# Order of the small matmuls in the head-group stage, and the queue that fetches its modulation weights

## The chip, the cores and the metric

The kernel runs on one core of a Trainium2 chip. The metric is device time in microseconds (us) of one execution. The engines are TensorE (PE, whose weight loads are listed as PEld), VectorE (DVE), ScalarE (ACT), GpSimd (POOL) and SyncE (SP, which here only issues DMAs; its issuing is listed as SPq). TensorE works on the data at the clock that the profile lists as granted, as a share of full speed.

## The reference

One layer of a decoder with a prompt of 512 tokens and eight single-token samples, width 2048, 32 heads of 64. Sixteen heads are dilated sliding-window softmax attention, sixteen are RWKV-7 heads. For the prompt an RWKV head runs this recurrence over all 512 tokens:

```
def step(S, inp):
    r_t, w_t, k_t, v_t, a_t, b_t = inp
    sa = jnp.einsum('bhij,bhj->bhi', S, a_t)
    S = S * w_t[:, :, None, :] + sa[..., None] * b_t[:, :, None, :] + v_t[..., None] * k_t[:, :, None, :]
    return S, jnp.einsum('bhij,bhj->bhi', S, r_t)
...
mix = jnp.concatenate([att, rw], axis=-1) @ P['w_out'][l]
x = x + gt1[:, None, :] * mix
h2 = modulate(rmsnorm(x, P['norm2_g'][l]), sh2, sc2)
```

Ahead of it stand a modulated norm and one input projection, behind it the output projection and a SwiGLU network. The factors `gt1`, `sh2`, `sc2` (and the rest of the modulation) are a projection of the condition `c` by `ada_w`, 2048 x 12288.

## The kernel before

The input projection, the output projection and the feed-forward network run as stages of their own. Between the first two lies the **head-group stage**, about 900 to 1527 us into the profiled execution. The change lies in it alone.

The stage treats heads in pairs, two heads on the two halves of 64 partitions: eight RWKV pairs and eight attention pairs. An RWKV pair (`rwkv_pair`) is cut into 8 chunks of 64 tokens. Its steps follow each other:

- `pg`: 16 matmuls of 64 rows give the products of every chunk's tokens (two banks of 512 columns for each head). VectorE masks each bank into `GM`.
- SyncE writes parts of `GM` to DRAM (`nd`) and reads them back in another layout (`i`). VectorE inverts all 16x16 diagonal blocks at once (`itmp`, `xi`, 19 instructions or so, each needing the last). SyncE writes the result to DRAM (`xd`) and reads it back as `XX`.
- GpSimd masks `E` out of `GM`. Then come short matmuls that double the block size of the inverse twice: `pq`, `px`, `pxt` (64x64, eight for each half) and `pq`, `px` with 32x32 blocks (in the program `pq2`, `px2`), with copies on ScalarE and sums on VectorE between them.
- `pat`, `pgv`, `pu`, `pxa` apply the inverse to the values and make the matrices `Mt` that carry the state from chunk to chunk.

The pair's `chain` then walks over the chunks (`pch`), and makes the outputs (`zy`, `z2`). An attention pair (`attn_pair`) computes scores `pz`, their transposes `pzt` and the values `po` of the prompt, and the samples' attention from the cache (`K` multiplied on GpSimd, `pov` on TensorE).

Beside this the stage makes the 16 blocks 8 to 23 of the modulation (`ada_steps`): each takes four transfers of 1 MiB of `ada_w` into one of two buffers `raw_ada`, 16 matmuls against `c_st`, and a sum. The call of `AQ.dma_start` at L236 issues the transfers; `AQ` is SyncE's queue.

A scheduler sets the order of each engine's instructions, from the order of calls (a string of steps such as `f2 r0 r1 c0 a0 f3 r2 c1`, where r is an RWKV pair, c its chain, a an attention pair and f some modulation blocks), and from when buffers come free; chains have a priority. The eight PSUM banks of the stage are divided up as: `pa` one bank (all `pg`), `psa` two (`pq` to `pxa`, used in turn), `pst` two (attention), one each for chains, samples and modulation. A matmul with 64 rows or 64 columns uses one half of the array. In the code a loop over `c` or `h` runs over the halves.

Of the kernel before, what the change touches and what calls it, by code (L numbers as in the profile page):

```python
# [12 lines left out]
ALU = mybir.AluOpType  # L13
# [65 lines left out]
def hymba_step(tc, a):  # L79
# [97 lines left out]
    with ExitStack() as top:  # L177
# [627 lines left out]
        with ExitStack() as wk_stack:  # L805
# [58 lines left out]
            copies = lambda name: wk.tile([P, 512], F32, tag="adac", name=name, bufs=1)  # L864
            todo += [ada_steps(b, raws, psd_, copies, SPL, PER) for b in range(ADA, ADB)]
# [13 lines left out]
            def rwkv_pair(pr):  # L879
# [88 lines left out]
                for c in range(2):  # L968
                    top_, bot = slice(c * 64, c * 64 + 32), slice(c * 64 + 32, c * 64 + 64)
                    for i in range(8):  # L970
                        mm(pq2[bot, i, :32], gm(i // 2, c, i % 2, top_, slice(c * 64 + 32, c * 64 + 64)), X2T[top_, i, :32])
                Q2 = tq2(f"Q2{pr}", 256).rearrange("p (i t) -> p i t", i=8)
                px2 = psa(f"px2{pr}").rearrange("p (i t) -> p i t", i=8)
                for c in range(2):
                    top_, bot = slice(c * 64, c * 64 + 32), slice(c * 64 + 32, c * 64 + 64)
                    ac.copy(Q2[bot], pq2[bot, :, :32])
                    for i in range(8):
                        mm(px2[top_, i, :32], Q2[bot, i, :], X2[bot, i, 32:])
                    ve.tensor_copy(X2[top_, :, 32:], px2[top_, :, :32])
# [11 lines left out]
                for c in range(2):  # L991
                    for b in range(4):
# [16 lines left out]
                Mt = wl.tile([P, 4, 2, E], F32, tag="mt", name=f"Mt{pr}", bufs=NMT)  # L1009
                for c in range(2):  # L1010
                    pxa = psa(f"pxa{pr}{c}")
                    for i in range(8):
                        o_ = i // 2 * 64
                        mm(pxa[hb[i % 2], o_ : o_ + 64], AG[hb[c], i, 1, :], X2[hb[c], i, :])
                    for i in range(8):
                        b, h = i // 2, i % 2
                        o_ = 256 + b * 64
# [448 lines left out]
```

## Time and profile before

| | us |
|---|---|
| median of three runs | 3356.26 |
| lowest and highest | 3343.64, 3372.01 |
| the profiled execution, its own time | 3378.55 |
| its span | 3376.8 |
| head-group stage in it | about 900 to 1527 |
| granted TensorE clock of the profiled execution, mean | 0.918 |

The profiled execution lies 22 us above the median of the runs, and its span lacks 1.8 us of its own time. TensorE is busy for 88% of the span, VectorE for 73%, ScalarE for 38%, GpSimd for 6%. A matmul is recorded as two or more passes, so a row's number of matmuls is twice that of the program's or more.

### The profile page before, as it was taken

What the parts mean: (1) busy time and instruction counts of PE and PEld (TensorE: products, weight loads), DVE (VectorE), ACT (ScalarE), POOL (GpSimd) and SP (SyncE); (2) the same over time, 40 slices, a digit from 0 to 9 for tenths busy, and PEclk for the clock granted to TensorE, in tenths of its full rate; (3) what the DMA queues carried; (4) which work ended last, traced back from release to release, by engine and by line L of the source; (5) the groups of instructions that cost most, each with busy time, mean ns of one, the idle gap of its engine ahead of it and who ended that gap; (6) DMA issues with size and microseconds to landing.
All of it is one profiled execution on the core that took longest, in us unless ns stands there. A gap on an engine that the chain in (4) does not pass through costs nothing.

```text
span 3376.8 us, 59004 instructions
## 1 busy us (share of the span) xinstructions
PE 2981.6 (88%) x23282; PEld 2629.4 (78%) x23282; DVE 2480.9 (73%) x4846; ACT 1278.0 (38%) x2041; POOL 212.9 (6%) x216
## 2 busy tenths in 40 slices
PE   6987888999889999977977999999999987888988
PEld 2477787889746666656967999999999987787878
DVE  5666788777557455656878787778777788889786
ACT  3353343334223343444434333333333343334333
POOL 0100122110012111101000000000000000000000
PEclk8978999999858798887988999999999998999999
DMA  7744444444579798933322333333333332323223
GB/s 255 232 139 154 147 159 157 133 146 140 175 223 282 201 239 232 249 103 117 109 78 69 113 104 104 108 112 107 113 101 113 109 125 96 99 94 119 85 94 104
DMA packets 449194, 476.17 MB, mean 141 GB/s; under 512 B 84110, under 2 KB 360547, under 8 KB 448916
## 3 DMA queue, kind: packets, MB, share of 16 engines
q1 hardware_dynamic: 438736, 452.16, 43.4%
q10 hardware_dynamic: 7428, 11.65, 1.0%
q0 software_dynamic: 2752, 8.60, 0.8%
q8 instruction: 182, 2.98, 0.4%
q14 instruction: 96, 0.79, 0.1%
HBM read 409.10 MB, written 68.17 MB: 141 GB/s over the span
## 4 chain that ended last, share of the span: by engine, by line
PE 35%; DVE 28%; DMA 23%; issue 5%; ACT 5%; SPq 1%; POOL 1%; ACTq 0%; DVEq 0%; POOLq 0%
PE ada L90 4%; DMA raw_ada<-in_ada_w 2%; SPq L130 1%; PE po L90 1%; DVE x_a L125 1%; PE lx L90 1%; PE pg L90 1%; PE pz L90 1%; PE px L90 1%; DMA K<-in_cache_k 1%; PE pch L90 1%; PE pq L90 1%; DMA xb<-in_ada_w 1%; PE q22M L90 1%; PE q31M L90 1%
## 5 line engine op out<-in xcount | busy, mean ns | idle before, releaser
L90 PE MATMUL ada<-raw_ada,c_st 128*32 128x512 f32 x584 | 123.7, 763 | 17.5 <-DMA raw_ada<-in_ada_w 16.8
L90 PE MATMUL ada<-xb,c_st 128*32 128x512 f32 x184 | 69.9, 673 | 15.9 <-DMA xb<-in_ada_w 13.8
L1037 ACT ACTIVATE Sall<-pch,ppl 64x64 f32<-64x64 f32 x128 | 39.5, 309 | 75.5 <-PE pch L90 57.7
L1238 POOL TENSOR_TENSOR K<-K,qb 128x1024 f32<-128x1024 f32 (+2 forms) x24 | 58.2, 2440 | 147.5 <-DMA K<-in_cache_k 91.6
L1188 ACT ACTIVATE z<-z,mx 128x128 f32<-128x128 f32 (+3 forms) x64 | 35.8, 560 | 78.2 <-DVE mx L1187 37.9
L90 PEld LDWEIGHTS pg<-AR,BK 64*128 64x128 f32 x256 | 41.0, 237 | 22.7 <-issue 11.9
L90 PE MATMUL pz<-ak,aq 64*128 64x256 f32 (+3 forms) x128 | 55.3, 581 | 0.7 <-DMA ak<-pqd 0.7
L90 PE MATMUL pg<-AR,BK 64*128 64x128 f32 x256 | 49.1, 342 | 6.1 <-DMA AR<-abd 2.7
L90 PE MATMUL g0M<-x_g,g0hl 128*128 128x260 f32 x168 | 31.3, 348 | 21.7 <-ACT x_g L124 7.4
L90 PE MATMUL po<-zt,av 128*64 128x128 f32 x320 | 49.1, 310 | 0.4 <-ACT zt L1200 0.4
L90 PE MATMUL o0M<-x_m,o0hl 128*128 128x260 f32 x168 | 33.5, 366 | 17.6 <-ACT x_m L124 14.2
L901 DVE TENSOR_TENSOR GM<-pg,cst 128x512 f32<-128x512 f32 x32 | 22.0, 688 | 36.5 <-PE pg L90 36.3
L198 PEld LDWEIGHTS pzt<-ident,z 128*128 128x128 f32 x160 | 19.0, 155 | 37.5 <-ACT z L1190 13.0
L1184 DVE SCALAR_TENSOR_TENSOR z<-pz,rnq,T 128x128 f32<-128x128 f32 (+3 forms) x64 | 34.4, 546 | 18.3 <-PE pz L90 16.2
L90 PEld LDWEIGHTS g0M<-x_g,g0hl 128*128 128x128 f32 x168 | 27.5, 241 | 25.4 <-ACT x_g L124 8.7
L90 PEld LDWEIGHTS o0M<-x_m,o0hl 128*128 128x128 f32 x168 | 29.7, 259 | 21.6 <-ACT x_m L124 17.5
L1412 DVE SCALAR_TENSOR_TENSOR y<-c_d,modT,y 128x512 f32<-128x512 f32 x64 | 45.9, 751 | 0.0
L90 PEld LDWEIGHTS ada<-raw_ada,c_st 128*32 128x32 f32 x584 | 16.4, 119 | 37.4 <-DMA raw_ada<-in_ada_w 22.7
L1200 ACT COPY zt<-pzt 128x128 f32<-128x128 f32 (+3 forms) x64 | 26.5, 426 | 49.5 <-PE pzt L198 41.1
L90 PEld LDWEIGHTS po<-zt,av 128*64 128x64 f32 x320 | 34.2, 151 | 13.3 <-issue 6.8
L198 PE MATMUL pzt<-ident,z 128*128 128x128 f32 x160 | 33.8, 321 | 11.8 <-ACT z L1190 10.0
L1190 ACT ACTIVATE z<-z,mx 128x128 f32<-128x128 f32 (+3 forms) x64 | 35.5, 559 | 16.8 <-DVE mx L1189 11.6
(2104 smaller groups left out, 9215.3 us busy)
## 6 DMA issues: line engine op xcount, KB each, us to landing
raw_ada<-in_ada_w SPq DMA_DIRECT2D x64, 1024.0 KB
xb<-in_ada_w SPq DMA_DIRECT2D x92, 256.0 KB
actd<-c_u SPq DMA_DIRECT2D x22, 520.0 KB
a<-actd SPq DMA_DIRECT2D x22, 520.0 KB
raw_ada<-in_ada_w SPq DMA_DIRECT2D x36, 256.0 KB
lsd<-lx SPq DMA_DIRECT2D x12, 520.0 KB
prd<-rkv SPq DMA_DIRECT2D x24, 256.0 KB
K<-in_cache_k SPq DMA_DIRECT2D x16, 384.0 KB
```

What stands on the lines that cost most here:

```text
L90: pe.matmul(out, lhsT=lhsT, rhs=rhs, start=start, stop=stop)
L125: ve.tensor_sub(x[:, 1, o:e], src, x[:, 0, o:e].bitcast(F32))
L130: sp.dma_start(raw.rearrange("p (k m) c -> p k (m c)", k=2), src[k * P : (k + 2) * P, :].rearrange("(k p) m -> p k m", p=P))
L198: pe.transpose(out, in_=in_, identity=ident[:n, 0:n])
L901: ve.tensor_tensor(GM[i][:, :, :, h], pg, gmask.unsqueeze(2).to_broadcast([P, 2, 2, P]), op=ALU.mult)
L1037: ac.activation(S[hb[h], ch + 1, hb[h]], pc_[hb[h], ch, :], AF.Copy, scale=ppl[hb[h], pr, ch : ch + 1])
L1184: ve.scalar_tensor_tensor(z, in0=pz[:, :nk], scalar=rn[:, qi, h : h + 1], in1=Ts[h][:, 384 - 128 * qi :], op0=ALU.mult, op1=ALU.add)
L1188: ac.activation(z, z, AF.Exp, bias=mx[:, 0:1], accum_out=mx[:, 1:2])
L1190: ac.activation(z, z, AF.Copy, scale=mx[:, 2:3])
L1200: ac.copy(zt, pzt[:, :nk])
L1238: OK.tensor_mul(K[:n], K[:n], qb[:n])
L1412: ve.scalar_tensor_tensor(y[:, f, :SEQ], in0=c[:, j, :SEQ], scalar=modT[:, 48 + f, 0:1], in1=y[:, f, :SEQ], op0=ALU.mult, op1=ALU.add)
```

## The change

Three things are different, all in the head-group stage.

1. The loops of most small matmuls are turned inside out, so that matmuls for the two halves follow each other in turn (`pg`, `pq`, `px`, `pxt`, `pq2`, `px2`, `pat`, `pgv`, `pu`, `pxa`, `z2`, `pz`, `po`). The number and sizes of matmuls stay as they are.
2. For that, two banks are needed at once where one was: `pg` of the second head comes from `psa` (`pa` still serves the first), both `pxa` banks are taken before the first `pxa` matmul, both `pz` before the first score.
3. `AQ` is GpSimd's queue from this stage on.

```
+            AQ = gp
             todo += [ada_steps(b, raws, psd_, copies, SPL, PER) for b in range(ADA, ADB)]
...
                 for i in range(2):
+                    pg = [f(f"pg{pr}{i}{h}").rearrange("p (b c t) -> p c b t", b=2, c=2) for h, f in enumerate((pa, psa))]
+                    for b in range(2):
+                        for c in range(2):
+                            cc = slice((4 * i + 2 * b + c) * 128, (4 * i + 2 * b + c + 1) * 128)
+                            for h in range(2):
+                                mm(pg[h][:, c, b, :], BK[hb[h], cc], AR[hb[h], cc])
                     for h in range(2):
-                        rows = slice(h * 64, h * 64 + 64)
-                        pg = pa(f"pg{pr}{i}{h}").rearrange("p (b c t) -> p c b t", b=2, c=2)
-                        for b in range(2):
-                            for c in range(2):
-                                cc = slice((4 * i + 2 * b + c) * 128, (4 * i + 2 * b + c + 1) * 128)
-                                mm(pg[:, c, b, :], BK[rows, cc], AR[rows, cc])
-                        ve.tensor_tensor(GM[i][:, :, :, h], pg, gmask.unsqueeze(2).to_broadcast([P, 2, 2, P]), op=ALU.mult)
+                        ve.tensor_tensor(GM[i][:, :, :, h], pg[h], gmask.unsqueeze(2).to_broadcast([P, 2, 2, P]), op=ALU.mult)
...
-                for c in range(2):
-                    for i in range(8):
+                for i in range(8):
+                    for c in range(2):
                         mm(pq[hb[c], i, :], E1f[hb[c], i, :], XX[1][hb[c], i, :])
...
+                pxa = [psa(f"pxa{pr}{c}") for c in range(2)]
+                for i in range(8):
+                    o_ = i // 2 * 64
+                    for c in range(2):
+                        mm(pxa[c][hb[i % 2], o_ : o_ + 64], AG[hb[c], i, 1, :], X2[hb[c], i, :])
...
                 def scores(qi):
                     nk = 128 * (qi + 1)
+                    pzs = [pst(f"pz{pr}{h}{qi}") for h in range(2)]
                     for h in range(2):
-                        hr = slice(h * 64, h * 64 + 64)
-                        pz = pst(f"pz{pr}{h}{qi}")
-                        mm(pz[:, :nk], q[hr, qi * 128 : (qi + 1) * 128], kn[hr, :nk])
+                        mm(pzs[h][:, :nk], q[hb[h], qi * 128 : (qi + 1) * 128], kn[hb[h], :nk])
+                    for h in range(2):
                         z = tz(f"z{pr}{h}{qi}", nk)
...
                     po = pst(f"po{pr}{qi}")
-                    for h in range(2):
-                        hr = slice(h * 64, h * 64 + 64)
-                        for j in range(qi + 1):
-                            mm(po[hr, :128], vt_[:, j, hr], zts[qi, h][:, j * 128 : (j + 1) * 128], start=(j == 0), stop=(j == qi))
+                    for j in range(qi + 1):
+                        for h in range(2):
+                            mm(po[hb[h], :128], vt_[:, j, hb[h]], zts[qi, h][:, j * 128 : (j + 1) * 128], start=(j == 0), stop=(j == qi))
```

The scheduler makes a new order for every engine out of this. The stage has 2,778 matmul instructions in both programs. Those whose predecessor uses a part of the array that they don't touch, before and after: `pq` (64x64) 11 and 120 of 128, `px` 12 and 124, `pxt` 3 and 126, `pgv` 16 and 123, `pu` 25 and 122, `pat` 10 and 56 of 64, `po` 24 and 119 of 160, `z2` 56 and 115 of 128. For `pg` it is 8 and 9 of 128 and for `pz` 21 and 20 of 64, so that these two stay as they were. The last of the 64 modulation transfers is used by the stage's 2,535th matmul before and by its 1,645th after.

On TensorE, where pair 0 ends and pair 1 is in its inversion, before (digits behind a name are the pair, then the bank and the head or half: `pg210` is pair 2, bank 1, head 0):

```order
L90 MATMUL pxa01_9440<-X20_9310,AG0_9366 64x64 x8
L90 MATMUL pxa01_9440<-BKt0_9353,XA0_9395 64x64 x8
L90 MATMUL ada10_10064<-sel4_67,adac10_10089 128x9 x4
L90 MATMUL pg210_10164<-AR2_10141,BK2_10142 128x128 x4
L90 MATMUL pz113_10747<-ak1_10646,aq1_10645 128x512
L198 MATMUL pzt102_10756<-ident_63,z102_10706 128x128 x3
L90 MATMUL pq1_9535<-XX11_9523,E11_9530 64x64 x8
L90 MATMUL pch0_9737<-Sall0_9132,Mt0_9420 64x64 x2
L90 MATMUL pq1_9535<-XX11_9523,E11_9530 64x64 x8
L90 MATMUL ada11_10096<-raw_ada11_0_10097,c_st_82 32x512 x4
L90 MATMUL ada11_10096<-raw_ada11_4_10103,c_st_82 32x512 x4
L90 MATMUL pg211_10170<-AR2_10141,BK2_10142 128x128 x4
```

The `pg` of pair 2 are done between the `pq` of pair 1. The same stretch of pair 2 after, at the end of pair 1:

```order
L90 MATMUL pxa11_9700<-BKt1_9631,XA1_9673 64x64
L198 MATMUL pzts1_10830<-ident_63,zs1_10825 97x16
L90 MATMUL ada14_10918<-raw_ada14_12_10937,c_st_82 32x512 x4
L90 MATMUL po20_11419<-zt210_11417,av2_11366 64x128
L90 MATMUL pz202_11423<-ak2_11365,aq2_11364 128x384
L90 MATMUL pov1_10839<-V10_10840,pts_10831 32x256 x4
L90 MATMUL pov1_10839<-V11_10846,pts_10831 32x256 x4
L90 MATMUL pov1_10839<-V12_10852,pts_10831 32x256 x4
L90 MATMUL pg201_10153<-AR2_10141,BK2_10142 128x128
L90 MATMUL pch1_10419<-Sall1_9133,Mt1_9698 64x64 x2
L90 MATMUL pg201_10153<-AR2_10141,BK2_10142 128x128 x3
L90 MATMUL pg211_10165<-AR2_10141,BK2_10142 128x128 x4
```

The second head's `pg` of pair 2 (`pg201`, `pg211`) now stand behind the last `pxa` of pair 1, since their bank is one of the two that pair 1 uses in turn up to `pxa`. In every later pair it is so too.

On VectorE, around the start of the 16x16 inversion of pair 4, before:

```order
L1062 TENSOR_TENSOR Y2_11325<-Y2_11325,z220_11335 128x256
L979 COPY X23_11092<-px23_11114 32x8x32
L926 TENSOR_TENSOR itmp4_11725<-i164_11721,xi4_11723 64x2
L928 TENSOR_REDUCE xi4_11723<-itmp4_11725 64x2
L926 TENSOR_TENSOR itmp4_11725<-i164_11721,xi4_11723 64x2x4
L928 TENSOR_REDUCE xi4_11723<-itmp4_11725 64x2x2
L926 TENSOR_TENSOR itmp4_11725<-i164_11721,xi4_11723 64x2x9
L1050 TENSOR_TENSOR UV2_10146<-UV2_10146,zy21_11345 64x2x128 x2
L928 TENSOR_REDUCE xi4_11723<-itmp4_11725 64x2x3
L979 COPY X23_11092<-px23_11114 32x8x32
L1270 COPY mixs_78<-pov2_11558 64x4 x4
L926 TENSOR_TENSOR itmp4_11725<-i164_11721,xi4_11723 64x2x16
```

Instructions of pair 2's chain, pair 3's inversion and the samples stand between those of the inversion. After:

```order
L902 TENSOR_TENSOR GM41_11692<-pg411_11706,cst_9118 128x4x128
L248 TENSOR_TENSOR modT_69<-ada21_12389,adab_72 128x36
L250 TENSOR_SCALAR modT_69<-modT_69 128x36
L1212 COPY at4_12809<-po43_12948 128x128
L927 TENSOR_TENSOR itmp4_11725<-i164_11721,xi4_11723 64x2
L929 TENSOR_REDUCE xi4_11723<-itmp4_11725 64x2
L927 TENSOR_TENSOR itmp4_11725<-i164_11721,xi4_11723 64x2x4
L929 TENSOR_REDUCE xi4_11723<-itmp4_11725 64x2x2
L927 TENSOR_TENSOR itmp4_11725<-i164_11721,xi4_11723 64x2x9
L929 TENSOR_REDUCE xi4_11723<-itmp4_11725 64x2x3
L927 TENSOR_TENSOR itmp4_11725<-i164_11721,xi4_11723 64x2x16
L929 TENSOR_REDUCE xi4_11723<-itmp4_11725 64x2x4
```

The inversion's instructions follow each other with nothing between.

On GpSimd, around the masking of `E` for pair 2 (`E12` in the rows), before:

```order
L1136 TENSOR_TENSOR tm3_10607<-T5_10542,dv_10550 128x1024
L1238 TENSOR_TENSOR K10_10805<-K10_10805,qb1_10801 128x1024
L1238 TENSOR_TENSOR K11_10811<-K11_10811,qb1_10801 96x1024
L1053 MEMSET Y1_10503 64x128
L948 TENSOR_TENSOR E12_10212<-GM20_10150,cst_9118 64x256
L948 TENSOR_TENSOR E12_10212<-GM21_10151,cst_9118 64x256
L948 TENSOR_TENSOR E12_10212<-GM20_10150,cst_9118 64x256
L948 TENSOR_TENSOR E12_10212<-GM21_10151,cst_9118 64x256
L1238 TENSOR_TENSOR K12_10817<-K12_10817,qb1_10801 97x1024
L1053 MEMSET Y2_11325 64x128
```

It stands among other multiplies and clears, and after it stands between DMA issues of `raw_ada`, each of which needs one of the two buffers to come free:

```order
L236 DMA raw_ada16_4_11612<-in_ada_w 128x4x512
L1243 TENSOR_TENSOR K22_11536<-K22_11536,qb2_11520 97x1024
L236 DMA raw_ada16_8_11618<-in_ada_w 128x4x512
L1059 MEMSET Y2_11325 64x128
L236 DMA raw_ada16_12_11624<-in_ada_w 128x4x512
L949 TENSOR_TENSOR E12_10212<-GM20_10150,cst_9118 64x256
L949 TENSOR_TENSOR E12_10212<-GM21_10151,cst_9118 64x256
L949 TENSOR_TENSOR E12_10212<-GM20_10150,cst_9118 64x256
L949 TENSOR_TENSOR E12_10212<-GM21_10151,cst_9118 64x256
L236 DMA raw_ada17_0_11638<-in_ada_w 128x4x512
```

The masks of `E` and the samples' multiplies `K` are now queued behind those issues.

## Rows read from the trace of the kernel before

**Rows 1.** The page's head: span of the profiled execution.

```profile
span 3376.8 us, 59004 instructions
```

**Rows 2.** Windows: stretch, length, busy PE, PEld, DVE, ACT, POOL, PEclk, DMA share, GB/s.

```profile
900.00:1520.00 620.00, 555.56 (x5251) 376.36 (x5251) 349.95 (x851) 230.43 (x615) 95.77 (x76) 0.79 0.79 222
915.00:1300.00 385.00, 348.80 (x3211) 232.17 (x3211) 223.90 (x538) 136.51 (x365) 66.27 (x51) 0.77 0.87 241
1200.00:1250.00 50.00, 45.75 (x473) 32.30 (x474) 27.77 (x70) 22.08 (x62) 10.47 (x8) 0.97 1.00 259
1373.00:1422.00 49.00, 44.58 (x517) 30.80 (x516) 31.77 (x77) 19.93 (x59) 10.86 (x9) 0.87 0.90 248
```

**Rows 3.** Timeline: last `Mt` of pairs 0 and 7.

```profile
1030.83 0.42 DVE L1020 TENSOR_TENSOR Mt<-pxa,eye 128x256 f32<-128x256 f32 x1
...
1481.74 0.42 DVE L1020 TENSOR_TENSOR Mt<-pxa,eye 128x256 f32<-128x256 f32 x1
```

**Rows 4.** Timeline of RWKV pair 6, from its last `pg` to its `Mt`.

```profile
1320.75 0.42 PE L90 MATMUL pg<-AR,BK 64*128 64x128 f32 x1
...
1325.47 0.60 SPq L915 DMA_DIRECT2D i<-nd  x1
...
1330.08 0.15 DVE L926 TENSOR_TENSOR itmp<-i,xi 64x2 f32<-64x2 f32 x1
...
1347.93 0.36 DVE L938 COPY xi<-xi 64x256 f32<-64x256 f32 x1
...
1349.29 0.84 SPq L941 DMA_DIRECT2D xd<-xi  x1
...
1361.81 4.60 SPq L944 DMA_DIRECT2D XX<-xd  x2
...
1421.95 0.42 DVE L1020 TENSOR_TENSOR Mt<-pxa,eye 128x256 f32<-128x256 f32 x1
```

**Rows 5.** Timeline, TensorE: start, length, engine, line, matmul, form, number of records.

```profile
1202.92 1.31 PE L90 MATMUL pu<-AG,X 64*64 64x128 f32 x14
...
1208.85 0.68 PE L90 MATMUL pxa<-X,AG 64*64 64x64 f32 x16
...
1209.37 0.46 PE L90 MATMUL pxa<-BKt,XA 64*64 64x64 f32 x10
...
1237.74 1.09 PE L90 MATMUL po<-zt,av 128*64 128x128 f32 x8
...
1248.01 0.70 PE L90 MATMUL pz<-ak,aq 64*128 64x256 f32 x2
...
1372.76 1.85 PE L90 MATMUL pq<-XX,E 64*64 64x64 f32 x32
...
1383.95 0.70 PE L90 MATMUL pz<-ak,aq 64*128 64x256 f32 x4
```

**Rows 6.** Groups of matmuls by form, 900 to 1520: busy, mean ns, idle before.

```profile
L90 PE MATMUL pg<-AR,BK 64*128 64x128 f32 x256 | 49.1, 342 | 6.1 <-DMA AR<-abd 2.7 <-DVE GM L901 2.1 <-DVE rb L857 0.8
L90 PE MATMUL po<-zt,av 128*64 128x128 f32 x320 | 49.1, 310 | 0.4 <-ACT zt L1200 0.4
L90 PE MATMUL px<-XX,Q 64*64 64x64 f32 x256 | 40.5, 267 | 0.1
L90 PE MATMUL pu<-AG,X 64*64 64x128 f32 x256 | 20.5, 275 | 0.0
```

**Rows 7.** Windows, VectorE's instructions on tile `xi` alone: busy, PEclk, DMA share, GB/s.

```profile
1330.00:1348.30 18.30, 8.11 (x19) 1.00 0.93 279
```

**Rows 8.** Waits of SyncE's queue, 900 to 1520: total, times, longest.

```profile
SPq L236 <- PE ada L90: 87.2, 28, 10.3
```

**Rows 9.** GpSimd's DMA issues of the next stage: duration ns min/median/max.

```profile
L1321 POOL DMA_DIRECT2D mix<-mixd x8: 722/722/790, 1529.1 to 1560.3; - x8
```

More of the change, by code (lines that the diff above doesn't have):

```diff
@@ L958, in rwkv_pair @@
                 pxt = psa(f"pxt{pr}").rearrange("p (i t) -> p i t", t=E)
-                for c in range(2):
-                    for i in range(8):
+                for i in range(8):
+                    for c in range(2):
                         mm(px[hb[c], i, :], Q[hb[c], i, :], XX[0][hb[c], i, :])
+                for i in range(8):
+                    for c in range(2):
                         mm(pxt[hb[c], i, :], XX[0][hb[c], i, :], Q[hb[c], i, :])
@@ L990, in rwkv_pair @@
                 pat = psa(f"pat{pr}")
-                for c in range(2):
-                    for b in range(4):
+                for b in range(4):
+                    for c in range(2):
                         mm(pat[hb[c], b * 128 : (b + 1) * 128], ARv[:, b, 3 * c, :], ident)
@@ L995, in rwkv_pair @@
                 pgv = psa(f"pgv{pr}")
-                for c in range(2):
-                    for i in range(8):
+                for i in range(8):
+                    for c in range(2):
                         mm(pgv[hb[c], i * 64 : i * 64 + 64], gm(i // 2, c, i % 2, hb[1 - c], hb[c]), UV[hb[1 - c], i // 2 * 2 + c, i % 2, :])
@@ L1002, in rwkv_pair @@
                     pu = psa(f"pu{pr}{q}").rearrange("p (b h x e) -> p b h x e", b=2, h=2, x=2)
-                    for c in range(2):
-                        for i in range(4):
+                    for i in range(4):
+                        for c in range(2):
                             mm(pu[hb[c], i // 2, i % 2], X2[hb[c], 4 * q + i, :], AG[hb[c], 4 * q + i])
@@ L1009, in rwkv_pair @@
                 Mt = wl.tile([P, 4, 2, E], F32, tag="mt", name=f"Mt{pr}", bufs=NMT)
-                for c in range(2):
[L1011 to L1017, printed above, removed]
-                        mm(pxa[hb[h], o_ : o_ + 64], XA[hb[c], b, h, :], BKt[hb[c], 2 * b + c, h * 64 : h * 64 + 64])
-                    ac.copy(ARv[:, :, 3 * c, :], pxa[:, :256].rearrange("p (b t) -> p b t", b=4))
-                    ve.tensor_tensor(Mt[:, :, c, :], pxa[:, 256:].rearrange("p (b t) -> p b t", b=4),
+                pxa = [psa(f"pxa{pr}{c}") for c in range(2)]
+                for i in range(8):
+                    o_ = i // 2 * 64
+                    for c in range(2):
+                        mm(pxa[c][hb[i % 2], o_ : o_ + 64], AG[hb[c], i, 1, :], X2[hb[c], i, :])
+                for i in range(8):
+                    b, h = i // 2, i % 2
+                    o_ = 256 + b * 64
+                    for c in range(2):
+                        mm(pxa[c][hb[h], o_ : o_ + 64], XA[hb[c], b, h, :], BKt[hb[c], 2 * b + c, h * 64 : h * 64 + 64])
+                for c in range(2):
+                    ac.copy(ARv[:, :, 3 * c, :], pxa[c][:, :256].rearrange("p (b t) -> p b t", b=4))
+                    ve.tensor_tensor(Mt[:, :, c, :], pxa[c][:, 256:].rearrange("p (b t) -> p b t", b=4),
                                      eye2.unsqueeze(1).to_broadcast([P, 4, E]), op=ALU.add)
@@ L1057, in chain @@
                     z2 = psz(f"z2{pr}{q}").rearrange("p (b e) -> p b e", b=4)
-                    for c in range(4):
+                    for n in range(8):
+                        c, h = n // 4 * 2 + n % 2, n // 2 % 2
                         b, R_ = 2 * q + c // 2, hb[1 - c % 2]
-                        for h in range(2):
-                            mm(z2[R_, c // 2, h * 64 : h * 64 + 64], gm(b, c % 2, h, slice(0, 128), R_), UV[:, 4 * q + c, h, :])
+                        mm(z2[R_, c // 2, h * 64 : h * 64 + 64], gm(b, c % 2, h, slice(0, 128), R_), UV[:, 4 * q + c, h, :])
                     ve.tensor_add(Y[:, q2], Y[:, q2], z2[:, :2])
@@ L1202, in values @@
                     po = pst(f"po{pr}{qi}")
-                    for h in range(2):
-                        hr = slice(h * 64, h * 64 + 64)
-                        for j in range(qi + 1):
-                            mm(po[hr, :128], vt_[:, j, hr], zts[qi, h][:, j * 128 : (j + 1) * 128], start=(j == 0), stop=(j == qi))
+                    for j in range(qi + 1):
+                        for h in range(2):
+                            mm(po[hb[h], :128], vt_[:, j, hb[h]], zts[qi, h][:, j * 128 : (j + 1) * 128], start=(j == 0), stop=(j == qi))
                     ve.tensor_copy(at[:, qi * 128 : (qi + 1) * 128], po[:, :128])
```

17 lines of the change are left out of this document (9 added, 8 removed).

## The prediction

> **What bounds the kernel now.** I read the page's head first [rows 1], then the windows of the head-group stage [rows 2], since the change lies there alone. From 900 to 1520 us TensorE is busy for 555.6 of 620 us at a mean granted clock of 0.79; VectorE is busy for 350, ScalarE for 230, GpSimd for 96, and the DMA engines for a share of 0.79. So TensorE is nearly full, and it is the first candidate. But it is nearly full with three kinds of work (RWKV pairs, attention, modulation) that cover each other's waits, and the stage also has a cadence: the last `Mt` of pair 0 is made at 1030.83 and that of pair 7 at 1481.74 [rows 3], which is 450.9 / 7 = 64.4 us for a pair. The third view is one pair's own path [rows 4]. In pair 6 the last `pg` ends at 1321.2, the first `pq` starts at 1372.8, and `Mt` is done at 1422.4: 51.6 us (call it L1) and 49.6 us (L2), together 101 us, though a pair comes every 64.4. Pairs overlap: while one is in its DMA round trips, the next has its `pg` done and its own inversion under way. That overlap, as much as TensorE's work, sets the stage's time.
>
> **The change part by part.**
>
> *Alternating halves.* In `pq`, 32 records of one half after another take 1.85 us, 57.8 ns each; `pxa`, which alternated already, starts 16 records between 1208.85 and 1209.37, 32.5 ns each [rows 5]. So a 64-column record that finds the other half free saves 25.3 ns. The order tells how many newly do: `pq`, `px`, `pxt` and `pgv` go from 42 to 493 of 512, which is 451 / 512 = 0.88 of 1,024 records (256 each, as `px` in [rows 6]): 1,024 x 0.88 x 25.3 ns = 22.8 us. `po`: 8 records in 1.09 us, 136 ns each [rows 5]; half of that saved in 95 / 160 of 320 records [rows 6]: 12.9 us. `pu`: 14 records in 1.31 us, 94 ns [rows 5], half saved in 97 / 128 of 256 [rows 6]: 9.1 us. `pat` and `z2` have no row of mine; between nothing and what `pu` saves a record (210 newly paired records x 47 ns = 9.9), I take 4. The sum is 49 us at full clock, and 49 / 0.79 = 62 us at the clock of the stage, if all of it lay on the path. The largest groups get nothing: `pg`, 49.1 us [rows 6], and `pz` have as many lone neighbours in the new order as before. For `pz` there was nothing to win: four records for both heads take 0.70 us, as two of one head do [rows 5].
>
> *The second bank.* `pg` of the second head now takes a bank of the pool that the inversion uses in turn from `pq` to `pxa`. The order shows the result: it stands behind the last `pxa` of the pair before. So `GM` of a pair, and all that follows, starts only when the pair before has finished: L1 and L2 of successive pairs no longer overlap, and the cadence becomes their sum. At today's values that is 101 us for each 64.4, so everything hangs on how much shorter L1 and L2 become when a pair is alone.
>
> The Trainium skill, page TensorEngine Tiling (Array Packing), section Gotcha 1: PSUM Pressure, states that row tiles write to different PSUM banks, and so raises what a kernel needs of them. That speaks against this change; the rows of `pz` are two heads in two banks, which agrees, and no row shows two row tiles in one bank. It gives no time.
>
> *L1 alone.* VectorE's 16x16 inversion takes from 1330.1 to 1348.3 [rows 4], of which 8.1 us are its own instructions [rows 7]; after, they stand without others between them: minus 10.2. Then `xd` is issued at 1349.3 and the last `XX` at 1361.8 [rows 4]. SyncE also has the modulation's transfers, whose waits for a buffer are 87.2 us in 28 cases, 3.1 us each [rows 8]; they go away from SyncE. One or two of them in these 12.5 us are 3 to 6 us; I take 5. On GpSimd the same waits now stand ahead of the masks of `E`, which `pq` needs too: 3.1 us more when one hits, nothing when `XX` is later anyway; I take 1.5. The issues themselves cost GpSimd some 0.72 us each, as those of the next stage do [rows 9], 64 x 0.72 = 46 us of an engine with 524 free [rows 2], hidden by that. L1 becomes 51.6 - 10.2 - 5 + 1.5 = 37.9; bounds 51.6 - 10.2 - 6.2 = 35.2 and 51.6 + 3.1 = 54.7.
>
> *L2 alone.* TensorE is busy for 44.6 of the 49 us of pair 6's L2 [rows 2], much of it with other work. What alternation saves in one pair is (22.8 + 12.9 + 9.1) / 8 / 0.87 = 6.4 us, so L2 is at most 49.6 - 6.4 = 43.2 if the other work stays among it. It is at least the pair's own matmuls: 312 of the 517 records there, by 1.85 us for 32 [rows 5], 18 us. Nothing in the trace says which; the window is shared with about one other pair, and half of that share should go. I take the middle, 30.6.
>
> *Sum.* 37.9 + 30.6 = 68.5 us for a pair, 4.1 more than 64.4, over seven intervals 29 us. Against the profiled execution's 3378.55 that is 3407; it lies 22 us above the median of the runs, so 3385 on their scale.
>
> *The modulation's transfers.* On their own queue they are no longer held back by SyncE's others; in the new order all 64 are used by the 1,645th of 2,778 matmuls, 22 more than had been by then. That is 23.1 MB, 89 us at the 259 GB/s that the DMA engines move at a share of 1.00 [rows 2]. Between 915 and 1300 they are free for 0.13 x 385 = 50 us [rows 2]. So up to 39 us are missing over the first 4.7 pairs, 8.3 each; the lower bound is nothing, if other transfers give way. Half of it, 4.2, is as large as the 4.1 that the pairs' own path adds, and runs beside it: I add nothing. If it did add, the time would be 20 to 39 us more, inside the range.
>
> **The rivals.**
>
> *TensorE is the bound, the pairs fit under it.* The decisive point is a sum of L1 and L2 under 64.4. TensorE busy at 0.90 speaks for it, and the low bounds, 35.2 + 18 = 53, lie under what TensorE then needs: 64.4 - 62 / 8 = 56.7 us. The stage saves all 62 us: 3378.55 - 62 - 22 = 3294. Against it: the new order leaves a lone pair's waits to be filled by attention and modulation, and uses the modulation up early. The Trainium skill, page TensorE: Matmul & The Clock Gate, section Part 3: Packing small matmuls — row/col tiling, has matmuls on different tiles of the array run side by side, started about 4 ns apart; by it halves in turn cost half, and this rival would be the result. The `pz` rows agree, and the `pxa` rows nearly (32.5 for 57.8, not 28.9). Chance 0.25.
>
> *A wash.* L1 and L2 come to 64 together, a mere 4 us under my sum, or the gain of TensorE outside the pairs (`po`, 12.9 us) comes through beside a small loss: 3378.55 - 22 = 3356. Chance 0.15.
>
> *Half the overlap's loss stays.* Other work still stands between a pair's steps, since attention and chains must be done some time: the cadence lies midway between 68.5 and the upper bounds' 54.7 + 43.2 = 97.9, at 83. That is 7 x 18.8 = 132 us more: 3488. Chance 0.17.
>
> *Serial at nearly the old latencies.* 97.9 for a pair, 7 x 33.5 = 235 more: 3591. TensorE would then stand idle for a third of the stage, which a scheduler with attention at hand should avoid. Chance 0.08.
>
> That the change doesn't do what it says is already in the sum for `pg` and `pz`.
>
> **How the numbers follow.** The forecast, 3385 (its own range 3365 to 3425, with the transfers' 39 at the top and three us less for a pair at the bottom), has 0.35. About 1%, 34 us, is what a measurement of this kernel can tell from no change, so faster means under 3323, slower over 3390. Faster is the first rival, 0.25. The wash and a little over half of the forecast's own range are within 1%: 0.15 + 0.18 = 0.33. Slower: the rest of the forecast and the two last rivals, 0.17 + 0.17 + 0.08 = 0.42. The range runs from 3285 (the first rival with 9 us more won) to 3490 (up to the midway case); left out are the serial case, half of the midway case and a little below the first rival, 0.08 + 0.08 + 0.04.
>
> **What would show it.** In the profile after: the `pg` of the second head should start after the `Mt` of the pair before; the inversion on VectorE should take 8 to 10 us in place of 18; L1 should be near 38 and L2 near 31, and the last `Mt` of the pairs 68 to 69 us apart. `pq` should show 32 records in about 1.04 us at full clock. Waits of SyncE at L236 should be gone, and GpSimd's should appear there; TensorE's idle time in the stage should grow from 64 us, with `pq<-XX` and `GM<-pg` as the instructions waited for. The prediction is wrong on the low side if L1 plus L2 is under 60, and on the high side if GpSimd's waits for a `raw_ada` buffer hold `E` back after `XX` has landed, or if TensorE waits for `raw_ada` itself in the first half of the stage.

## The result and the profile after

The changed kernel takes 3474.09 us (median of four runs, 3454.11 to 3481.31) beside 3364.14 us of the kernel before on the same occasions: ratio 1.0325, interval 1.0277 to 1.0373, some 109 us more. Executions over 1.5% above their kernel's fastest, of which there are two in one run, are left out of every time below. The profiled execution has a span of 3469.3 us, against 3376.8 [rows 1].

Its windows, with columns as in [rows 2], show the whole head-group stage (which now ends near 1620), and the stretches from the `Mt` of pair 0 to that of pair 4, and from there to that of pair 7:

```profile
900.00:1620.00 720.00, 532.94 (x5289) 335.21 (x5287) 345.12 (x860) 230.51 (x626) 139.41 (x142) 0.72 0.66 193
1003.00:1387.00 384.00, 291.28 (x2884) 168.68 (x2881) 195.39 (x459) 119.30 (x323) 93.51 (x94) 0.78 0.80 241
1387.00:1570.00 183.00, 146.26 (x1631) 109.28 (x1629) 90.12 (x245) 71.01 (x193) 23.18 (x23) 0.70 0.33 84
```

TensorE has less to do and waits more: 533 us busy of 720, where [rows 2] had 556 of 620. Four pairs take 384 us in the first stretch, 96 each, three take 183 in the second, 61 each. The DMA share is 0.80 in the first and 0.33 in the second. The mean granted clock of the stage fell as well, from 0.79 to 0.72. It is lower in the second stretch (0.70) than in the first (0.78), so it is not what makes the first four pairs long; how much of the whole loss it carries was not measured.

The timeline of the changed kernel, `Mt` of pairs 0, 2 and 7, and the `pg` that follows pair 2's:

```profile
1002.16 0.76 DVE L1026 TENSOR_TENSOR Mt<-pxa,eye 128x256 f32<-128x256 f32 x2 [0.50 <-ACT AR L1025]
...
1204.34 0.76 DVE L1026 TENSOR_TENSOR Mt<-pxa,eye 128x256 f32<-128x256 f32 x2 [4.57 <-ACT AR L1025]
1205.68 2.07 PE L90 MATMUL pg<-AR,BK 64*128 64x128 f32 x8
...
1568.95 0.76 DVE L1026 TENSOR_TENSOR Mt<-pxa,eye 128x256 f32<-128x256 f32 x2 [8.96 <-ACT AR L1025]
```

The last `pg` of pair 3 runs at 1205.7, as soon as pair 2's `Mt` is out of the way: pairs stand one behind the other. In every pair from 1 on the last `pg` ends between 4.4 us before and 3.5 us after the `Mt` of the pair before it, where it ended 38 to 102 us ahead of it in the kernel before. The cadence from pair 0 to pair 7 is (1569.3 - 1002.5) / 7 = 81.0 us, against 64.4 in [rows 3].

Pair 6 of the changed kernel, step by step as in [rows 4]:

```profile
1447.39 0.93 PE L90 MATMUL pg<-AR,BK 64*128 64x128 f32 x6
...
1458.29 0.60 SPq L916 DMA_DIRECT2D i<-nd  x1
...
1463.62 0.15 DVE L927 TENSOR_TENSOR itmp<-i,xi 64x2 f32<-64x2 f32 x1
...
1473.42 0.37 DVE L939 COPY xi<-xi 64x256 f32<-64x256 f32 x1
1474.64 2.96 SPq L945 DMA_DIRECT2D XX<-xd  x4
...
1479.44 0.44 PE L90 MATMUL pq<-XX,E 64*64 64x64 f32 x2 [4.05 <-DMA XX<-xd]
...
1515.83 0.42 DVE L1026 TENSOR_TENSOR Mt<-pxa,eye 128x256 f32<-128x256 f32 x1
```

L1 (end of `pg` to `pq`) is 31 us and L2 (to `Mt`) 37, where [rows 4] had 51.6 and 49.6. VectorE's inversion takes 10.2 us in place of 18. Pair 3 of the same kernel, in the first stretch:

```profile
1205.68 2.07 PE L90 MATMUL pg<-AR,BK 64*128 64x128 f32 x8
...
1222.09 0.60 SPq L916 DMA_DIRECT2D i<-nd  x1
...
1234.36 0.15 DVE L927 TENSOR_TENSOR itmp<-i,xi 64x2 f32<-64x2 f32 x1
...
1242.59 0.37 DVE L939 COPY xi<-xi 64x256 f32<-64x256 f32 x1
1247.17 5.12 SPq L945 DMA_DIRECT2D XX<-xd  x4
...
1258.01 0.44 PE L90 MATMUL pq<-XX,E 64*64 64x64 f32 x2 [1.45 <-DMA XX<-xd]
...
1301.36 0.76 DVE L1026 TENSOR_TENSOR Mt<-pxa,eye 128x256 f32<-128x256 f32 x2 [1.25 <-ACT AR L1025]
```

The inversion is even a little shorter (8.6 us), yet L1 is 50 us and L2 44. The longer part is what lies around the inversion: from the issue of `i` to its use 12.3 us in place of 5.3, from the inversion's end to `pq` 15 in place of 6. There are round trips through DRAM in these steps, but they are not all of it. VectorE's last wait before `itmp` is for a matmul of a chain, and `itmp` follows without a wait for `i`:

```profile
1233.30 0.72 DVE L1056 TENSOR_TENSOR UV<-UV,zy 64x128 f32<-64x128 f32 x2 [7.13 <-PE zy L90]
```

In pair 4 both kinds stand side by side. `itmp` waits 8 us for `i`; later the last `XX` is issued at 1335, and TensorE, before it comes to `pq`, stands still for a `raw_ada` buffer:

```profile
1320.40 0.15 DVE L927 TENSOR_TENSOR itmp<-i,xi 64x2 f32<-64x2 f32 x1 [7.95 <-DMA i<-nd]
...
1343.28 1.93 PE L90 MATMUL ada<-raw_ada,c_st 128*32 128x512 f32 x6 [6.52 <-DMA raw_ada<-in_ada_w]
...
1348.99 1.18 PE L90 MATMUL pq<-XX,E 64*64 64x64 f32 x26
```

Groups of matmuls by form, of the same stage, as in [rows 6]:

```profile
L90 PE MATMUL po<-zt,av 128*64 128x128 f32 x320 | 39.8, 329 | 0.0
...
L90 PE MATMUL pq<-XX,E 64*64 64x64 f32 x256 | 15.7, 282 | 13.2 <-DMA XX<-xd 13.2
L90 PE MATMUL px<-XX,Q 64*64 64x64 f32 x256 | 12.1, 256 | 2.8 <-ACT Q L957 2.7
```

Alternating halves does what it says: `po` takes 39.8 us for 49.1. `px` shows 12.1 for 40.5, but that is not its own gain alone: before, `px` and `pxt` stood among each other, so that each row also held time of the other. The windows of all matmuls that read `XX` (`pq`, `px`, `pxt` of 64x64 together), before and after, count every stretch once:

```profile
900.00:1533.00 633.00, 65.79 (x768) 0.79 0.78 219
900.00:1620.00 720.00, 38.26 (x768) 0.72 0.66 193
```

That is 38.3 us for 65.8. And `pq` now waits for `XX`, which it hardly did before. The waits of TensorE and of GpSimd (engine, line, released by: total, times, longest):

```profile
PE ada L90 <- DMA raw_ada<-in_ada_w: 54.7, 16, 12.2
...
POOL raw_ada L236 <- PE ada L90: 230.4, 50, 13.4
```

GpSimd now holds the waits for a `raw_ada` buffer, and TensorE waits for the modulation's weights for 54.7 us, against 15.2 in the kernel before.

### The profile page after: what moved, and what is told of

Read it like the earlier page. It is cut to its first block, busy times and chain, and to the rows that moved or that the text cites. A ratio compares the mean times of both kernels' runs of the same rounds, so it can differ in the third digit from the quotient of the medians.

```text
span 3469.3 us, 59042 instructions
## 1 busy us (share of the span) xinstructions
PE 2957.8 (85%) x23282; PEld 2592.2 (75%) x23282; DVE 2473.4 (71%) x4846; ACT 1274.3 (37%) x2041; POOL 256.1 (7%) x280
## 4 chain that ended last, share of the span: by engine, by line
PE 24%; DVE 24%; DMA 20%; issue 4%; ACT 4%; SPq 1%; ACTq 0%; DVEq 0%; POOL 0%; POOLq 0%
DMA raw_ada<-in_ada_w 2%; PE ada L90 2%; PE pg L90 1%; DVE x_a L125 1%; SPq L130 1%; DMA BK<-abd 1%; DMA XX<-xd 1%; DMA K<-in_cache_k 1%; DMA i<-nd 1%; PE pch L90 1%; PE pz L90 1%; PE q31M L90 1%; PE po L90 1%; PE o1M L90 1%; PE q32M L90 1%
## 5 line engine op out<-in xcount | busy, mean ns | idle before, releaser
L236 POOL DMA_DIRECT2D raw_ada<-in_ada_w x64 | 48.7, 761 | 255.9 <-PE ada L90 230.4
L1243 POOL TENSOR_TENSOR K<-K,qb 128x1024 f32<-128x1024 f32 (+2 forms) x24 | 56.2, 2350 | 53.0 <-DMA K<-in_cache_k 49.6
L90 PE MATMUL pz<-ak,aq 64*128 64x128 f32 (+3 forms) x128 | 52.7, 559 | 4.2 <-DVE at L1212 2.5
L90 PE MATMUL pg<-AR,BK 64*128 64x128 f32 x256 | 45.0, 338 | 10.2 <-DMA BK<-abd 6.4
L1244 DVE TENSOR_REDUCE lg<-K 128x16 f32<-128x1024 f32 (+2 forms) x24 | 29.0, 1210 | 30.9 <-POOL K L1243 30.9
L1212 DVE COPY at<-po 128x128 f32<-128x128 f32 x32 | 9.2, 288 | 52.5 <-PE po L90 52.4
L902 DVE TENSOR_TENSOR GM<-pg,cst 128x512 f32<-128x512 f32 x32 | 21.9, 688 | 31.8 <-PE pg L90 31.6
L198 PE MATMUL pzt<-ident,z 128*128 128x128 f32 x160 | 36.3, 338 | 6.6 <-ACT z L1196 3.9
L90 PE MATMUL po<-zt,av 128*64 128x128 f32 x320 | 39.8, 329 | 0.0
```

Source lines behind the costliest of these rows:

```text
L90: pe.matmul(out, lhsT=lhsT, rhs=rhs, start=start, stop=stop)
L198: pe.transpose(out, in_=in_, identity=ident[:n, 0:n])
L236: AQ.dma_start(raw, src if per == 1 else src.rearrange("(j p) c -> p j c", p=P))
L1243: OK.tensor_mul(K[:n], K[:n], qb[:n])
L1244: ve.tensor_reduce(lg[:n, i, :], K[:n].rearrange("p (g e) -> p g e", e=E), axis=AX.X, op=ALU.add)
```

## The experiments

Three theories stood at first. Theory 1: the second bank of `pg`, which is one of the two that the inversion uses in turn, makes pairs serial, and that alone costs the time. Theory 2: GpSimd's queue costs it. Theory 3: the alternating order, with its two banks at once for `pxa` and `pz`, costs it.

**Only the queue moved**, on the kernel before:

```
+            AQ = gp
             todo += [ada_steps(b, raws, psd_, copies, SPL, PER) for b in range(ADA, ADB)]
```

> The kernel before with only the queue of the modulation weights moved to GpSimd. Theory 1 (the second pg bank makes the RWKV pairs serial, and that alone costs the time): the pairs overlap as before, last Mt of successive pairs 62 to 68 us apart, 3340 to 3400 us. Theory 2 (GpSimd's queue costs it: waits for a raw_ada buffer stand ahead of the masks of E and the samples' multiplies): about as slow as the changed kernel, 3440 us or more. Theory 3 (alternating and taking two pxa and two pz banks at once costs it): as before, 3350 to 3380 us.

3362.88 us, ratio 0.995 (0.9918 to 0.9982). The queue alone costs nothing, so theory 2 falls; the last `Mt` of pairs are 60 us apart on the mean, a little under the 62 to 68 expected. Pairs overlap as before. That they are closer than the 64.4 us of the kernel before may lie in the execution alone: its profile is 22 us above the median of its runs.

**Everything but the queue**:

```
-            AQ = gp
             todo += [ada_steps(b, raws, psd_, copies, SPL, PER) for b in range(ADA, ADB)]
```

> The changed kernel with the modulation weights on SyncE's queue, everything else as changed. Theory 1: about as slow as the changed kernel, 3440 to 3520 us, pairs serial with last Mt 75 to 90 us apart; waits for raw_ada back on SyncE may add some us. Theory 2: the loss goes, 3300 to 3380 us. Theory 3: as slow as the changed kernel, too.

3476.59 us, ratio 1.0288 (1.0237 to 1.0339), pairs 80.3 us apart: as slow as the changed kernel, as theories 1 and 3 have it.

**`pg` back in one bank**, the rest as changed:

```
+                    for h in range(2):
+                        rows = slice(h * 64, h * 64 + 64)
+                        pg = pa(f"pg{pr}{i}{h}").rearrange("p (b c t) -> p c b t", b=2, c=2)
...
-                    pg = [f(f"pg{pr}{i}{h}").rearrange("p (b c t) -> p c b t", b=2, c=2) for h, f in enumerate((pa, psa))]
...
```

> The changed kernel with only the pg loop as before (both heads in the pa bank, one after the other); all other loops alternate, and GpSimd fetches the modulation weights. Theory 1: pairs overlap again and the 62 us of TensorE's saved time come through in part: 3290 to 3345 us. Theory 2: 3400 us or more, since the queue stays on GpSimd. Theory 3: 3440 us or more, since the banks of pxa and pz are still taken two at a time.

3337.95 us, ratio 0.9876 (0.9828 to 0.9924). The loss is gone, and theory 3 with it: all other loops alternate here, with two banks at once for `pxa` and `pz`.

**The same with SyncE's queue** (the edit above, and `AQ = gp` taken out):

> The changed kernel with the pg loop as before and the modulation weights on SyncE's queue: only the alternating of the other loops is left of the change. Theory 1: 3290 to 3345 us, as the run that keeps GpSimd's queue, within 20 us of it. Theory 2: 3290 to 3345 us, and clearly faster than that run. Theory 3: 3440 us or more.

3330.25 us, ratio 0.9846 (0.9798 to 0.9894); it is the fastest kernel of this study, some 52 us under the kernel before. The intervals of the two runs overlap, so the queue shows no difference here either. The last `Mt` of pairs 0 and 7 in the timeline of this run:

```profile
1019.49 0.75 DVE L1025 TENSOR_TENSOR Mt<-pxa,eye 128x256 f32<-128x256 f32 x2
...
1408.75 0.75 DVE L1025 TENSOR_TENSOR Mt<-pxa,eye 128x256 f32<-128x256 f32 x2 [0.45 <-ACT AR L1024]
```

Pairs are (1409.1 - 1019.9) / 7 = 55.6 us apart. In its windows TensorE is busy for 483 us of the stage, at a granted clock of 0.81:

```profile
900.00:1468.00 568.00, 483.32 (x5286) 311.46 (x5286) 334.12 (x858) 227.56 (x624) 93.90 (x78) 0.81 0.85 244
```

**Only the second bank**, on the kernel before:

```
-                        pg = pa(f"pg{pr}{i}{h}").rearrange("p (b c t) -> p c b t", b=2, c=2)
+                        pg = (pa, psa)[h](f"pg{pr}{i}{h}").rearrange("p (b c t) -> p c b t", b=2, c=2)
```

> The kernel before with only the bank of the second head's pg taken from the inversion's pool (psa); no loop alternates, SyncE fetches the modulation weights. Theory 1: the whole loss, without the gain: pairs serial, 3490 to 3560 us. If the loss needs the alternating order or the two pxa banks as well: 3400 us or less.

3501.28 us, ratio 1.0398 (1.034 to 1.0456). One name in one line costs about 134 us. From the timeline of this run:

```profile
1004.65 0.42 DVE L1020 TENSOR_TENSOR Mt<-pxa,eye 128x256 f32<-128x256 f32 x1
...
1593.46 0.42 DVE L1020 TENSOR_TENSOR Mt<-pxa,eye 128x256 f32<-128x256 f32 x1 [0.93 <-ACT AR L1019]
```

That is 84.1 us a pair, 95.8 in the first four and 68.5 in the last three. Theory 1 is shown: the bank alone has the whole loss.

Open was then why serial pairs take 81 us each and not the 68.5 that I had forecast, and why the first four take so much longer than the last three. The modulation's last matmul with `raw_ada` starts at 1352 us, close to where the pairs get fast.

**The changed kernel without the modulation's transfers**: two pieces are fetched once, and all 16 blocks are computed from them. So it leaves out 62 of the 64 transfers, and its results are not the layer's.

```
+                if fetch:
+                    AQ.dma_start(raw, src if per == 1 else src.rearrange("(j p) c -> p j c", p=P))
...
+            rawc = [wk.tile([P, PER, 512], F32, tag="rawa", name=f"rawc{i}", bufs=NRA) for i in range(2)]
+            for i in range(2):
+                sp.dma_start(rawc[i], ada_w[i * PER * P : (i + 1) * PER * P, ADA * 512 : ADA * 512 + 512].rearrange("(j p) c -> p j c", p=P))
+            raws = lambda name, g: [rawc[g // PER % 2]]
```

> The changed kernel, but the stage's modulation weights are fetched only twice (one 1 MiB piece into each of the two buffers), and all 16 blocks are computed from these two pieces; so 62 of 64 transfers and all waits for them are left out. Theory 1a (the loss is the latency of pairs that stand one behind the other): last Mt of successive pairs still 68 us or more apart, 3400 to 3470 us, at least 60 us more than the kernel before without the transfers. Theory 1b (the loss is the modulation's transfers crowded into the first half, which the serial order lets run ahead): pairs 55 to 64 us apart from the first, 3280 to 3340 us, within 30 us of the kernel before without the transfers.

**The kernel before without them** (the same edit):

> The kernel before with the same transfers left out (two pieces fetched, 62 transfers left out), to set beside the changed kernel without them. Either theory: a little under the kernel before, 3320 to 3365 us, since TensorE waited for raw_ada only some 15 us there.

The first takes 3402.4 us, ratio 1.0117 (1.0071 to 1.0163), the second 3358.17, ratio 0.9987 (0.9953 to 1.0021). So leaving the transfers out gains the kernel before nothing that can be measured, and the changed kernel 0.0325 - 0.0117, 2.1% or 70 us. Of the expected numbers, theory 1a's time and spacing were met, but not its 60 us over the kernel before without transfers: 44 us remain between these two kernels, and both causes are at work. In the timeline of the changed kernel without transfers:

```profile
991.36 0.41 DVE L1032 TENSOR_TENSOR Mt<-pxa,eye 128x256 f32<-128x256 f32 x1
...
1502.17 0.76 DVE L1032 TENSOR_TENSOR Mt<-pxa,eye 128x256 f32<-128x256 f32 x2 [10.19 <-ACT AR L1031]
```

Pairs are 73 us apart. The same steps as for pairs 3 and 6 above, taken from the timelines of one execution each, as means over pairs in us:

| step | changed, pairs 1 to 4 | changed, pairs 5 to 7 | without transfers, pairs 1 to 4 |
|---|---|---|---|
| last `pg` to issue of `i` (mask, `nd` written) | 15.2 | 9.1 | 12.9 |
| issue of `i` to first `itmp` | 9.1 | 4.9 | 4.5 |
| inversion on VectorE | 14.9 | 9.2 | 17.2 |
| end of it to last `XX` issued (`xd` written) | 6.9 | 3.8 | 5.2 |
| last `XX` issued to `pq` | 9.0 | 2.5 | 3.4 |
| L2 | 41.6 | 31.8 | 37.6 |

The four steps with a round trip (rows 1, 2, 4 and 5) sum to 40.2, 20.3 and 26.0 us. With the other two rows pairs 1 to 4 are longer by 14.2 - 2.3 + 4.0 = 15.9 us each with the transfers, 64 us together; the last three pairs of the run without transfers are slower, 199 us for 183. `E` is not to blame: its mask was done 5.9 to 19.8 us ahead of `pq` in every pair of the changed kernel.

How the 70 us come about stays open. Three things in these steps differ between the two kernels. Landing takes longer: `i` of pair 4 lands 9.5 us after its issue, where no pair without transfers took more than 7.2 to `itmp`. TensorE waits for `raw_ada`: of the 54.7 us, 23 lie in pairs 1 to 4 between the last `XX` and `Mt`, and `pq` of pairs 1, 2 and 4 starts without any wait for `XX`. And the modulation's matmuls stand elsewhere: without transfers the last one starts at 1160 us in place of 1352, and between the `Mt` of pairs 2 and 4 there are 10 of the 512 records in place of 176. Other serial runs with all transfers have four-step sums of 38.2 (everything but the queue) and 30.6 us (only the second bank) in pairs 1 to 4, so that one execution's 40.2 is not to be taken for a fixed price.

**One `raw_ada` buffer** in place of two, so that the transfers can't run ahead:

```
-            NTA, NTB, NTC, NZ, NL, NKV, NRA = 6, 5, 5, 6, 2, 3, 2
+            NTA, NTB, NTC, NZ, NL, NKV, NRA = 6, 5, 5, 6, 2, 3, 1
```

> The changed kernel with one raw_ada buffer in place of two, so that the modulation's transfers can't run ahead: in the built order 39 of 64 pieces are used by the 1,645th matmul, in place of all 64, and pairs stay serial. All transfers are made. If the crowded transfers make up half of the loss (as the run without them says): last Mt of pairs 72 to 76 us apart, with no long first four, 3400 to 3430 us. If it was only the waits for raw_ada, and not when the transfers come: no gain, since every piece now waits for the one buffer, 3470 us or more.

3499.32 us, ratio 1.0414 (1.0356 to 1.0471): no gain, and pairs 87.8 us apart. The waits of TensorE in this run:

```profile
PE ada L90 <- DMA raw_ada<-in_ada_w: 92.5, 24, 12.6
```

The edit doesn't tell the two apart as I had meant: TensorE waits more, and the transfers go on through all eight pairs (the last three 81 us apart) in place of the first five.

**Half pieces**: the same bytes in 128 transfers of 0.5 MiB into four buffers.

```
-            NPS, NPA, NPT, NPG, SP, SPL, PER = 1, 2, 2, 1, 1, 8, 4
+            NPS, NPA, NPT, NPG, SP, SPL, PER = 1, 2, 2, 1, 1, 8, 2
...
-            NTA, NTB, NTC, NZ, NL, NKV, NRA = 6, 5, 5, 6, 2, 3, 2
+            NTA, NTB, NTC, NZ, NL, NKV, NRA = 6, 5, 5, 6, 2, 3, 4
```

> The changed kernel with the modulation's weights fetched in 128 pieces of 0.5 MiB into four buffers, the same bytes in the same memory; the built order is otherwise nearly that of the changed kernel. If TensorE's waits for raw_ada come from the bytes that must arrive in the first half: same waits, within 20 us of the changed kernel, 3455 to 3495 us. If they come from the grain of two large buffers: the waits halve, 3420 to 3450 us.

3483.41 us, ratio 1.0349 (1.0301 to 1.0396): the changed kernel's time. But the waits of TensorE nearly halve:

```profile
PE ada L90 <- DMA raw_ada<-in_ada_w: 30.0, 16, 9.6
```

So both expectations were wrong in part: the waits went with the grain, and the time didn't go with the waits. Pairs are 80.2 us apart. In pairs 1 to 4 the four steps fell to 34.2 us and L2 rose to 46.2. So fewer waits for `raw_ada` alone gain nothing; that these waits are slack isn't shown, since in pair 4 above one stands right ahead of `pq`.

**`pg`'s second bank from the attention's pool**:

```
-                    pg = [f(f"pg{pr}{i}{h}").rearrange("p (b c t) -> p c b t", b=2, c=2) for h, f in enumerate((pa, psa))]
+                    pg = [f(f"pg{pr}{i}{h}").rearrange("p (b c t) -> p c b t", b=2, c=2) for h, f in enumerate((pa, pst))]
```

> The changed kernel, but pg of the second head takes its bank from the attention's pool of two (pst) in place of the inversion's (psa). Theory 1: pairs overlap, 3290 to 3345 us, near the run with pg in one bank. If any second bank for pg costs, whatever its pool: 3400 us or more.

3387.41 us, ratio 1.0036 (1.0011 to 1.0061), pairs 69.3 us apart. Between the two expectations: much of the loss goes, but not all. The last pair's `pg` ends at 1394.9 us, against 1312.4 with one bank; that this pool's turns tie `pg` to the attention is the likely reason, and no run shows it by itself.

**Two banks of its own for `pg`**, with the modulation's sums in the samples' bank to make room, and SyncE's queue:

```
-            NPS, NPA, NPT, NPG, SP, SPL, PER = 1, 2, 2, 1, 1, 8, 4
+            NPS, NPA, NPT, NPG, SP, SPL, PER = 1, 2, 2, 2, 1, 8, 4
...
-            psd_ = lambda name: psB.tile([P, 512], F32, tag="psd", name=name, bufs=1)
+            psd_ = pss_
...
-            AQ = gp
...
-                    pg = [f(f"pg{pr}{i}{h}").rearrange("p (b c t) -> p c b t", b=2, c=2) for h, f in enumerate((pa, psa))]
+                    pg = [f(f"pg{pr}{i}{h}").rearrange("p (b c t) -> p c b t", b=2, c=2) for h, f in enumerate((pa, pa))]
```

> The changed kernel with SyncE's queue, and two banks of their own for pg (the modulation's sums share the samples' bank to make room for it). In the built order pg now alternates in 73 of 127, and pg runs ahead of the pair before. If the pool of the second bank was what was wrong with it: 3290 to 3340 us, up to 20 us under the run with pg in one bank on SyncE's queue, since half of pg's 49 us pair up in part. If giving the modulation and the samples one bank costs as much: 3340 to 3380 us.

3406.97 us, ratio 1.0126 (1.0079 to 1.0173): a loss against one bank for `pg`, beyond either expectation. Pairs are 63.9 us apart; TensorE waits 47.3 us for `raw_ada`. The edit changes two pools, and which of them costs is not told apart by it.

**Only the RWKV pairs' loops alternate** (`pg` in one bank, SyncE's queue, `scores` and `values` as before):

```
-                    pzs = [pst(f"pz{pr}{h}{qi}") for h in range(2)]
                     for h in range(2):
-                        mm(pzs[h][:, :nk], q[hb[h], qi * 128 : (qi + 1) * 128], kn[hb[h], :nk])
...
+                        pz = pst(f"pz{pr}{h}{qi}")
+                        mm(pz[:, :nk], q[hr, qi * 128 : (qi + 1) * 128], kn[hr, :nk])
...
-                    for j in range(qi + 1):
-                        for h in range(2):
...
+                    for h in range(2):
...
+                        for j in range(qi + 1):
...
```

> The run with pg in one bank on SyncE's queue, but the attention's loops (pz, po) as before, so that only the RWKV pairs' matmuls alternate. If TensorE's saved time counts at the clock of the stage wherever it is saved (the prediction's sum: inversion 45 of 62 us, po 16): 35 to 45 us under the kernel before, 3315 to 3335 us, some 10 to 16 us over the run with po too. If only the pairs' own path counts: no slower than that run. If only time off the pairs' path counts: within 15 us of the kernel before.

3353.18 us, ratio 0.9963 (0.9934 to 0.9991), some 12 us under the kernel before, as the third expectation has it. The windows of the stage in this run, in the kernel before, and in the run with only the queue moved:

```profile
900.00:1494.00 594.00, 496.48 (x5288) 317.52 (x5286) 350.15 (x858) 230.82 (x625) 98.15 (x78) 0.81 0.81 234
900.00:1533.00 633.00, 560.90 (x5284) 378.44 (x5284) 351.43 (x858) 232.24 (x623) 97.29 (x78) 0.79 0.78 219
900.00:1509.00 609.00, 538.89 (x5284) 365.61 (x5284) 337.62 (x859) 230.94 (x625) 144.24 (x142) 0.83 0.77 227
```

TensorE is busy for 496 us, 64 less than in the kernel before and 42 less than in the run with only the queue moved. The last two have the same matmul loops and differ by 22 us of busy time at granted clocks of 0.79 and 0.83, so a saving read from one profile is no surer than that. Either way most of the saved TensorE time is here, and little of the gain in time; `po` and `pz` bring 13 us less of busy time and the other 40 us. So the third expectation's number came out, but its reason, that only time off the pairs' path counts, isn't shown: whether it is `po` itself or the whole new order that the scheduler then makes is not settled.

## Why the prediction came out as it did

The direction, the serial pairs and the range were right; the forecast's own value (3385) was 89 us too low. The time lies outside the forecast's own range, which ended at 3425, and near the third rival's 3488. That the whole range holds it is partly luck: its upper end was priced by that rival, and most of what a pair took beyond the forecast goes with the transfers, which the sum put at nothing.

Alternating `pq` in the run with one bank and SyncE's queue, on which the second point rests:

```profile
1254.30 1.10 PE L90 MATMUL pq<-XX,E 64*64 64x64 f32 x30
```

- *The second bank makes pairs serial.* Right, and shown by undoing it both ways: it costs 134 us by itself (only the bank), 149 with the other loops alternating (ratio 1.0288 against 0.9846, on SyncE's queue), 151 on GpSimd's (1.0325 against 0.9876).
- *Alternating halves, 62 us if all lay on the path.* The cost of a record at full clock was nearly right, 36.7 ns for the 32.5 taken: 30 records of `pq` take 1.10 us. TensorE's busy time in the stage is 78 us less in that run than in the kernel before and 56 less than in the run with only the queue moved, and 52 us of time came through. The forecast had it spread as 45 for the inversion and 16 for `po`; measured were 12 and 40. In serial pairs it gave less: only the bank 1.0398, with the alternating 1.0288, 37 us.
- *L1 and L2 of a lone pair, 37.9 and 30.6.* Both terms were too small: the means of pairs 1 to 7 of the changed kernel are 44.1 and 37.4, together 13 us more than the forecast's 68.5. Pair 6, from which L1 was taken, has the shortest L1 of the kernel before, 51.6 us where the mean of pairs 1 to 7 is 71.6. Without transfers the means are 37.4 and 36.3. That L1 then agrees is partly luck: the inversion took 13.9 us on the mean there, not 8, and the steps around it were shorter by about as much. In the changed kernel the inversion ran in 8 to 10 us as said, except in pair 1 (27), where VectorE also had the samples' state update, and pair 2 (15). From the inversion's end to the last `XX` it took 6.9 us (pairs 1 to 4) and 3.8 (5 to 7), for 13.5 and more in [rows 4], a larger gain than the 5 I took. But it is not the queue's: with the transfers on SyncE's queue (everything but the queue) it is 6.9 and 4.6.
- *The modulation's transfers: "I add nothing".* This is the term that was most wrong. I had them wait beside the pair's path and priced the missing bandwidth, at most 39 us, as hidden. Leaving them out takes 70 us off the serial kernel. The sign that the prediction named for the high side was there: TensorE waits for `raw_ada`, 54.7 us, most of it in the first half of the stage and some right ahead of a pair's own matmuls. In the kernel before leaving out the same transfers gains nothing (0.9987), though its four steps, too, take 62.8 us with them and 32.1 without (pairs 1 to 4): pairs overlapped there, so that another pair's work could cover that.
- *The queue.* Costs on GpSimd were put at 1.5 us a pair, and none can be measured; the expected hazard, `E` held back, didn't come.
- *The rivals.* The first, "TensorE is the bound", named 56.7 us a pair, and the run with one bank came to 55.6. That TensorE was its bound isn't shown: it was busy for 0.85 of that stage, 483 us of 568, and the runs above gave 12 us of time for most of the saved TensorE time. The Trainium skill, page TensorE: Matmul & The Clock Gate, section Part 3: Packing small matmuls — row/col tiling, has matmuls on different tiles side by side; the records agree in kind (`pq`, `px` and `pxt` 38.3 us for 65.8, not quite the half), and the result went the other way all the same, because of where the banks came from. The midway rival named 83 us a pair, and 81.0 were measured; without the transfers it is 73, so 8 of the 12.5 us beyond 68.5 go with them. How much of it is other work between a pair's steps, as that rival had it, the runs don't separate.

## What to carry to other kernels

A bank (or buffer) taken from a pool that is used in turn carries that pool's whole order with it: ask whose last use frees it, and whether two pieces of work that ran beside each other now stand one behind the other. Where overlap goes away, price a path's lone latency from more than one of its instances and with the transfers that will run at the same time, since overlap had been hiding both. A part of an edit that helps (alternating halves, here 1.5%) may be buried under another part that it doesn't need; time the parts apart.

## What was not expected of the hardware

The four steps of a pair that hold round trips through DRAM, of 64 and 128 KB, took 40.2 us in pairs 1 to 4 while 1 MiB transfers were under way (DMA share 0.80 over the stretch), and 26.0 in the same pairs without them. Part of that is landing time, such as the 8 us that VectorE waited for `i` in pair 4, and part is the engines' own order. Cutting those transfers in half pieces left pairs as far apart (80.2 us for 81.0). A wait of 54.7 us that stands at the top of TensorE's list was nearly halved without any gain. And the same matmuls kept TensorE busy for longer where pairs stood one behind the other: 533 us at a mean granted clock of 0.72 in the changed kernel, 483 at 0.81 with `pg` in one bank.
